# Attention scores of a two-layer trunk: the low part of q on 128 rows beside zeros, and outputs stored block by block

## The chip, the cores and the metric

The kernel runs on one core of one Trainium2 chip. The metric is device time in microseconds (us) for one execution; lower is better. Engines are named as the profile names them: PE is the tensor engine (PEld its weight loads), DVE the vector engine, ACT the scalar engine, POOL GpSimd, SP the engine whose queue (SPq) issues nearly all DMAs here.

## The reference

Two layers over 1024 tokens of 1024 features, each a mixer and then a squared-ReLU MLP with norms around them. The change lies in the scores of two of the four mixers:

```python
def diff_attention(q, k, v, lam, subln_w, rel_bias, layer_idx):      # layer 0: 8 heads, 2 maps of 64 features
    ...
        logits = jnp.einsum("bqhmd,bkhmd->bhmqk", q_blk, k32) + bias[None, :, None]
        logits = jnp.where(dist >= 0, logits, -jnp.inf)
        p = jax.nn.softmax(logits, axis=-1)
        attn = p[:, :, 0] - lam_full * p[:, :, 1]
        return jnp.einsum("bhqk,bkhe->bqhe", attn, v32)
...
def sliding_window_attention(q, k, v, sinks, rel_bias):              # layer 1: 8 heads of 64 features, window 128
    ...
    logits = jnp.einsum("bnqgrd,bnkgd->bngrqk", q32, kb) + bias
```

Everything is fp32. The other two mixers (a state-space scan beside the differential attention, retention beside the sliding window), the projections and the MLPs are untouched.

## The kernel before

A product in fp32 accuracy is made of three products of a faster type: each operand is split into a high part (hi) and the exact rest (lo), and the sum has hi times hi, hi times lo and lo times hi. In the projections (`fm_unit`, L410 to L412, and `tok_unit`, L496 to L498) these are three matmuls on 128 rows with 512 or 256 columns.

A score has only 64 features to contract, so `qk` (L552 to L557) does with two matmuls. `q_stack` (L533) writes hi of q for map m to both halves of the partitions of `qh[:, m]`; `k_stack` (L544) writes hi of k to the map's own 64 partitions and lo of k to the other 64. The first matmul (L555) contracts 128 rows: q hi with k hi and k lo together. The second (L557) has q lo, which stands on the map's own 64 partitions of `ql`, against the hi part of k on the same 64 partitions: it contracts 64 rows. Both accumulate in one tile of PSUM, `psc` in differential attention and `pswa` in the sliding window.

Differential attention (L881 to L943) goes over 8 heads and in each over 8 query blocks of 128, from the last to the first. A block with nk keys has, for each of its 2 maps, one pair of such matmuls for every 512 keys or the rest of them (L903 to L906); then DVE adds the bias and takes the maximum (L909), ACT takes the exponential (L912), DVE joins the maps (L922), PE transposes the result (L929), DVE or ACT copies it to `aT` (L931), PE multiplies by the values (L935), and DVE scales the block into `ys` (L941). `ys` holds all 8 blocks of a head, in slot 16 or 17, and one DMA stores it at the head's end (L943). The `psc` tiles have two buffers of two banks. The projections of the next head and the values of the next pair of heads are issued among the blocks.

The sliding window (L1033 to L1085) goes over 4 pairs of heads and 8 blocks each, with 128 or 256 keys per block, 2 maps, and one matmul pair per map; its outputs were always stored block by block (L1085). There too projections of later heads stand between the blocks.

Each engine's order is set when the program is built: the tile framework places instructions by their dependencies and by when it expects buffers to come free, and then every engine and the SP queue run their list in order. Slots 0 to 19 are 4 KB per partition each and are handed on from phase to phase. GpSimd takes the lo parts of the weights in differential attention and in the sliding window (`lo_on`, L881, L1032, `split_w`, L158).

Of the kernel before, what the change touches and what calls it, by code (L numbers as in the profile page):

```python
# [9 lines left out]
F32 = mybir.dt.float32  # L10
# [18 lines left out]
def trunk(ctx: ExitStack, tc: tile.TileContext, x, c, rel_bias, norm_gains, mod_w, mod_b, mlp_w1, mlp_w2,  # L29
# [13 lines left out]
    def open_wide(shape, bufs):  # L43
        """The other four banks: as two tiles of two banks, or as four of one."""
        if wide:
            wide["stack"].close()
        wide["stack"] = ExitStack()
        wide["pool"] = wide["stack"].enter_context(tc.tile_pool(name="pw", bufs=bufs, space=PSUM, reuse_waits="tile"))
        wide["shape"] = shape
# [10 lines left out]
    def turn(i):  # L60
        """0 and 1 by turns, for each i."""
        turns[i] = 1 - turns.get(i, 1)
        return turns[i]

    def slot(i, shape, dtype=F32, name="slot"):
        """A tile of up to 4 KB in slot i of 20, which the phases of the kernel hand on one by one."""
# [6 lines left out]
    # k_mat: identity, upper triangle (t <= l), strict lower (t > s), ones  # L73
# [29 lines left out]
    def load_cols():  # L103
        """Vectors by feature: cols[:, 0] gains (8 + 8 s), mod_b (40 + 16 s), conv bias (104), SSD norm (120);
        cols[:, 1] conv taps, and the norm of differential attention (64)."""
# [23 lines left out]
    def rstd_of(ss, n, tag="rstd", post=None):  # L129
        """(ss / n + EPS) ** -0.5 on small tiles."""  # L130
# [18 lines left out]
    def split_w(shape, src):  # L149
        """hi by the scalar engine (the next spare[0] by GpSimd), lo by the engine of lo_on."""  # L150
# [16 lines left out]
    def load_fm(w, c0, nft, given=None):  # L167
        """Blocks [128, 8 k, 128 cols] for feature-major products; yields nft (hi, lo) pairs."""
# [10 lines left out]
    def load_group(w, r0):  # L179
        """512 rows of w [*, 1024]: (hi, lo) pairs [128, 2 f, 512] by (f pair, column half)."""  # L180
# [37 lines left out]
    def mod_first(s, after_load, after):  # L218
        """Shift and scale of the first sublayer, 256 columns of each at a time."""
# [7 lines left out]
        for cp in range(4):  # L227
# [11 lines left out]
            # the shift on the tensor engine, as a row; the scale on the vector engine  # L239
# [65 lines left out]
    def col_tasks(s):  # L305
        st = {}

        def fin_t(which):
            def fin(acc):
                col = stat.tile([P, 8], F32, tag=f"col{which}", name="col", bufs=1)  # L310
                parts = split_acc(acc)
                for cc in range(2):
# [3 lines left out]
                    # every row has all the sums: keep the diagonal of each block  # L316
# [10 lines left out]
    xd = {s: dp.tile([NT, P, D], F32, tag=f"xd{s}", name=f"xd{s}") for s in range(3)}  # L327

    class Flow:
        """The residual stream between two sublayers: Y by token tile, u by pairs (hi, lo)."""  # L330
# [23 lines left out]
    def pre_norm(yp, t, xsrc):  # L354
        """Y[t] <- xsrc * rstd(xsrc)."""
# [6 lines left out]
    def post(yp, t, s):  # L362
        """x_new = x + gate * rms(Y) * g_post."""
# [20 lines left out]
    def hT_cols(yp, hf, s, h, ks):  # L384
        """Transposes features ks of the four token tiles of a half, applies (a, b) of sublayer s, splits hi / lo."""
# [18 lines left out]
    def fm_unit(blk, hf):  # L404
        """psum[128 cols, 512 tok] = (W block)^T h of one half."""
# [9 lines left out]
    def out_unit(yp, us, blks, t, cc, first):  # L415
        """Y[t][:, half cc] (+)= sum over 4 f-tiles of u^T w; us[hf][f] = (hi, lo)."""
# [70 lines left out]
    def tok_unit(blks, t, n, ps=None):  # L487
        """psum[128 tok, n cols] = h W for one token tile; blks = [(k0, nk, (hi, lo))]."""
# [24 lines left out]
    def proj_fm(w, c0, nft, evac, early=False, hfs=(0, 1), given=None):  # L513
        """Feature-major product; early: only the first half of the tokens now, the second by what it returns."""
# [13 lines left out]
    def silu2(th, dst, src):  # L528
        """dst = 2 silu(src)."""
# [3 lines left out]
    def q_stack(q, sl, ps):  # L533
        """q = (qh, ql): qh[:, m] has the hi part of one 64-row half of psum / 8 on both halves of the partitions,
        ql the lo parts of the two in place."""
        qh, ql = q
        for m in range(2):
# [3 lines left out]
            nc.vector.scalar_tensor_tensor(out=ql[own, sl], in0=ps[own, :], scalar=0.125,  # L541
# [733 lines left out]
```

## Time and profile before

| | us |
|---|---|
| median of 3 runs | 3244.49 |
| lowest and highest run | 3241.71, 3244.67 |
| span of the profiled execution | 3244.0 |
| differential attention with what is interleaved (480 to 1035) | 555 |
| sliding window with what is interleaved (1953 to 2130) | 177 |

The profiled execution has a span of 3244.0 us, 0.5 us under the median of the runs. The two stages are stretches of that span, from about the first to the last score product of each.

### The profile page before, as it was taken

To read this page: it belongs to the slowest core of one execution; us is meant where nothing else is said; L and a number is where in the kernel's file an instruction comes from. 1 tells how busy PE (TensorE), PEld (TensorE's weight loads), DVE (VectorE), ACT (ScalarE), POOL (GpSimd) and SP (SyncE) were. 2 spreads that over 40 slices of the span, in tenths; PEclk is the share of its full clock that TensorE was granted. 3 is DMA by queue.
4 is the path that set the end of the run, shared out by engine and by line. 5 is a ranking of instruction groups with operands and counts; after the bars stand their busy time and mean duration, and the time that the engine had idled before them with its cause. 6 is when DMAs were issued, how large, how long until landed. Compare 5 with 4: busy or idle time off the path is not lost.

```text
span 3244.0 us, 39799 instructions
## 1 busy us (share of the span) xinstructions
PE 3179.3 (98%) x16018; PEld 2619.1 (81%) x16018; DVE 1696.5 (52%) x3001; ACT 1061.3 (33%) x2041; POOL 456.1 (14%) x414
## 2 busy tenths in 40 slices
PE   8999999999999999999999999999999999999999
PEld 5888887877777878888888878899988788888887
DVE  5788875545675564444433454545455544333334
ACT  4323335444442251112212265432223522111112
POOL 0334442121100120000000142011102100000003
PEclk9999999999999999999999999999999999999999
DMA  6232311111132232322111142233233322111112
GB/s 201 72 101 77 98 53 38 38 54 41 37 143 85 84 124 71 98 91 91 58 47 52 65 146 67 76 109 107 79 130 112 116 78 71 33 47 52 52 52 91
DMA packets 180156, 262.56 MB, mean 81 GB/s; under 512 B 8713, under 2 KB 144514, under 8 KB 179074
## 3 DMA queue, kind: packets, MB, share of 16 engines
q1 hardware_dynamic: 179584, 259.90, 24.5%
q8 instruction: 126, 2.06, 0.3%
q14 instruction: 60, 0.49, 0.0%
q10 hardware_dynamic: 386, 0.11, 0.0%
HBM read 226.95 MB, written 33.03 MB: 80 GB/s over the span
## 4 chain that ended last, share of the span: by engine, by line
PE 86%; DVE 7%; DMA 3%; ACT 2%; issue 1%; POOL 0%; SPq 0%; POOLq 0%; ACTq 0%; DVEq 0%
PE pg L410 11%; PE pg L411 11%; PE pg L412 11%; PE pg L422 10%; PE pg L424 10%; PE pg L423 10%; PE pg L496 4%; PE pg L498 3%; PE pg L497 3%; PE psc L557 2%; PE pav L935 2%; PE psc L555 1%; DVE ch L765 1%; PE pat L929 1%; DMA xt<-xd 1%
## 5 line engine op out<-in xcount | busy, mean ns | idle before, releaser
L410 PE MATMUL pg<-hh,wh 128*128 128x512 f32 x1760 | 693.0, 395 | 5.8 <-ACT hh L393 2.8
L411 PE MATMUL pg<-hl,wh 128*128 128x512 f32 x1760 | 692.9, 394 | 0.1
L412 PE MATMUL pg<-hh,wl 128*128 128x512 f32 x1760 | 692.4, 393 | 0.0
L422 PE MATMUL pg<-wh,u 128*128 128x512 f32 x1472 | 588.0, 400 | 3.1 <-DVE Y L431 2.2
L424 PE MATMUL pg<-wh,u 128*128 128x512 f32 x1472 | 583.6, 397 | 0.0
L423 PE MATMUL pg<-wl,u 128*128 128x512 f32 x1472 | 581.5, 395 | 0.2 <-DVE wl L158 0.2
L156 ACT CAST wh<-raw 128x1024 fp32r<-128x1024 f32 (+1 forms) x246 | 257.3, 1049 | 797.9 <-PE pg L424 546.7
L410 PEld LDWEIGHTS pg<-hh,wh 128*128 128x128 f32 x1760 | 330.6, 188 | 79.8 <-ACT hh L393 4.2
L412 PEld LDWEIGHTS pg<-hh,wl 128*128 128x128 f32 x1760 | 330.9, 188 | 70.3 <-issue 2.1
L411 PEld LDWEIGHTS pg<-hl,wh 128*128 128x128 f32 x1760 | 331.1, 188 | 69.6 <-issue 2.3
L158 DVE TENSOR_TENSOR wl<-raw,wh 128x1024 fp32r<-128x1024 f32 (+1 forms) x194 | 238.1, 1230 | 256.4 <-ACT wh L156 256.3
L422 PEld LDWEIGHTS pg<-wh,u 128*128 128x128 f32 x1472 | 277.8, 189 | 69.1 <-DVE Y L431 4.1
L431 DVE TENSOR_TENSOR Y<-pg,Y 128x512 f32<-128x512 f32 x264 | 181.9, 689 | 290.0 <-PE pg L424 287.6
L424 PEld LDWEIGHTS pg<-wh,u 128*128 128x128 f32 x1472 | 277.4, 189 | 66.4 <-issue 0.6
L423 PEld LDWEIGHTS pg<-wl,u 128*128 128x128 f32 x1472 | 277.9, 189 | 64.1 <-DVE wl L158 0.5
L496 PE MATMUL pg<-wh,hh 128*128 128x256 f32 (+1 forms) x992 | 292.5, 295 | 13.7 <-DVE zs L531 11.5
L498 PE MATMUL pg<-wh,hl 128*128 128x256 f32 (+1 forms) x992 | 288.4, 291 | 0.6 <-DVE hl L395 0.6
L497 PE MATMUL pg<-wl,hh 128*128 128x256 f32 (+1 forms) x992 | 288.5, 291 | 0.0
L368 POOL TENSOR_TENSOR yg<-Y,gg 128x512 f32<-128x512 f32 x36 | 54.8, 1522 | 1344.0 <-DVE Y L431 1343.0
L496 PEld LDWEIGHTS pg<-wh,hh 128*128 128x128 f32 x992 | 192.6, 194 | 18.5 <-DVE zs L531 10.9
L498 PEld LDWEIGHTS pg<-wh,hl 128*128 128x128 f32 x992 | 192.2, 194 | 4.8 <-issue 1.4
L497 PEld LDWEIGHTS pg<-wl,hh 128*128 128x128 f32 x992 | 192.7, 194 | 3.1 <-issue 1.0
(327 smaller groups left out, 3906.3 us busy)
## 6 DMA issues: line engine op xcount, KB each, us to landing
raw<-in_mlp_w_dram SPq DMA_DIRECT2D x64, 1024.0 KB, 5.3
raw<-in_mod_w_dram SPq DMA_DIRECT2D x40, 1024.0 KB, 5.0
raw<-in_e_w_in_dram SPq DMA_DIRECT2D x32, 512.0 KB, 4.0
xd<-xt SPq DMA_DIRECT2D x24, 512.0 KB, 2.6
xt<-xd SPq DMA_DIRECT2D x24, 512.0 KB, 4.3
raw<-in_e_w_in_dram SPq DMA_DIRECT2D x10, 1024.0 KB, 5.5
raw<-in_e_w_out_dram SPq DMA_DIRECT2D x10, 1024.0 KB, 5.6
raw<-in_o_w_in_dram SPq DMA_DIRECT2D x9, 1024.0 KB, 5.2
```

The lines of the kernel that those rows point to most:

```text
L156: nc.scalar.copy(out=wh, in_=src)
L158: lo_on[0].tensor_tensor(out=wl, in0=src, in1=wh.bitcast(F32), op=ALU.subtract)
L410: mm(ps, lhsT=wh[:, k], rhs=hh[:, k], start=(k == 0), stop=False)
L411: mm(ps, lhsT=wh[:, k], rhs=hl[:, k], start=False, stop=False)
L412: mm(ps, lhsT=wl[:, k], rhs=hh[:, k], start=False, stop=(k == 7))
L422: mm(ps, lhsT=uh[:, tl], rhs=wh[:, f % 2], start=(f == 0), stop=False)
L423: mm(ps, lhsT=uh[:, tl], rhs=wl[:, f % 2], start=False, stop=False)
L424: mm(ps, lhsT=ul[:, tl], rhs=wh[:, f % 2], start=False, stop=(f == 3))
L431: nc.vector.tensor_tensor(out=dst, in0=ps, in1=dst, op=ALU.add)
L496: mm(ps[:, 0:n], lhsT=hh[:, k, tl], rhs=wh[:, i], start=(k == 0), stop=False)
L497: mm(ps[:, 0:n], lhsT=hh[:, k, tl], rhs=wl[:, i], start=False, stop=False)
L498: mm(ps[:, 0:n], lhsT=hl[:, k, tl], rhs=wh[:, i], start=False, stop=(k == 7))
```

## The change

The second score product contracts 128 rows: each map has its own `ql` tile, with the lo part of q on the map's 64 partitions and zeros on the other 64, and the stationary and moving operands of L557 become whole 128-partition slices. `q_tiles` clears the other half with a GpSimd memset of 64 partitions by 1024 columns, twice per head in differential attention and twice per pair of heads in the sliding window (24 in all). In differential attention the second `ql` tile takes slots 16 and 17; `ys` becomes a tile of one block with three buffers, stored at each block (64 stores of 128 by 128 instead of 8 of a whole head), and `aT` has three buffers instead of four. In the sliding window the second `ql` tile takes slot 15 or the buffer `macc`, which is otherwise the accumulator of the modulation vectors. Comments and docstrings are gone too, so lines after L556 have other numbers.

```diff
     def q_stack(q, sl, ps):
...
-            nc.vector.scalar_tensor_tensor(out=ql[own, sl], in0=ps[own, :], scalar=0.125,
+            nc.vector.scalar_tensor_tensor(out=ql[m][own, sl], in0=ps[own, :], scalar=0.125,
                                            in1=qh[own, m, sl].bitcast(F32), op0=ALU.mult, op1=ALU.subtract)
...
         qh, ql = q
         mm(ps, lhsT=qh[:, m, qsl], rhs=ks[:, ksl], start=True, stop=False)
-        rows_ = slice(m * 64, m * 64 + 64)
-        mm(ps, lhsT=ql[rows_, qsl], rhs=ks[rows_, ksl], start=False, stop=True)
+        mm(ps, lhsT=ql[m][:, qsl], rhs=ks[:, ksl], start=False, stop=True)
+
+    def q_tiles(qh, ql):
+
+        for m in range(2):
+            nc.gpsimd.memset(ql[m][64 - m * 64:128 - m * 64, :].bitcast(F32), 0.0)
+        return [(qh[i], [t[:, i * 512:i * 512 + 512] for t in ql]) for i in range(2)]
...
-                places = ((12, 13, 2, 3, 4), (19, 18, 14, 15, 5))[h % 2]
-                ql = slot(places[4], [P, D], F32R, "ql")
-                q = [(slot(places[2 * i], [P, 2, 512], F32R, "qh"), ql[:, i * 512:i * 512 + 512]) for i in range(2)]
+                places = ((12, 13, 2, 3, 4, 16), (19, 18, 14, 15, 5, 17))[h % 2]
+                q = q_tiles([slot(places[2 * i], [P, 2, 512], F32R, "qh") for i in range(2)],
+                            [slot(places[4 + m], [P, D], F32R, "ql") for m in range(2)])
...
-                ys = slot(16 + h % 2, [P, 8, P], F32, "ys")
...
-                        aT = mp.tile([P, 4, P], F32, tag="aT", name="aT", bufs=4)
+                        aT = mp.tile([P, 4, P], F32, tag="aT", name="aT", bufs=3)
...
-                    nc.vector.tensor_scalar(out=ys[:, qb], in0=po[:, 0:P], scalar1=r, scalar2=rc[:, 0:1],
+                    ys = mp.tile([P, P], F32, tag="ys", name="ys", bufs=3)
+                    nc.vector.tensor_scalar(out=ys, in0=po[:, 0:P], scalar1=r, scalar2=rc[:, 0:1],
                                             op0=ALU.mult, op1=ALU.mult)
-                nc.sync.dma_start(out=yd[2 + h // 4][:, :, (h % 4) * P:(h % 4 + 1) * P], in_=ys)
+                    nc.sync.dma_start(out=yd[2 + h // 4][:, qb, (h % 4) * P:(h % 4 + 1) * P], in_=ys)
...
-                ql = slot(places[2], [P, D], F32R, "ql")
-                q = [(slot(places[n], [P, 2, 512], F32R, "qh"), ql[:, n * 512:n * 512 + 512]) for n in range(2)]
+                lo1 = slot(15, [P, D], F32R, "ql") if i % 2 == 0 else const.tile([P, D], F32R, tag="macc", name="ql")
+                q = q_tiles([slot(places[n], [P, 2, 512], F32R, "qh") for n in range(2)],
+                            [slot(places[2], [P, D], F32R, "ql"), lo1])
```

What the program's order becomes is shown at three places. The first is PE in the second head of differential attention, before the change (score products L555 and L557, values times probabilities L935, projections L410 to L412, a transposition L929; a size is that of the output):

```order
L555 MATMUL psc<-ks,qh 128x512
L557 MATMUL psc<-ks,ql 128x512
L935 MATMUL pav<-v,aT 128x128 x2
L555 MATMUL psc<-ks,qh 128x512
L557 MATMUL psc<-ks,ql 128x512
L410 MATMUL pg<-hh_595,wh 128x512
L555 MATMUL psc<-ks,qh 128x512
L557 MATMUL psc<-ks,ql 128x512
L555 MATMUL psc<-ks,qh 128x384
L929 MATMUL pat<-kmat,p 128x128
L557 MATMUL psc<-ks,ql 128x384
```

The same place on PE with the change (L556 is the second product, L939 and L933 are what were L935 and L929):

```order
L555 MATMUL psc<-ks,qh 128x512
L556 MATMUL psc<-ks,ql 128x512
L939 MATMUL pav<-v,aT 128x128 x2
L555 MATMUL psc<-ks,qh 128x512
L556 MATMUL psc<-ks,ql 128x512
L410 MATMUL pg<-hh_595,wh 128x512
L555 MATMUL psc<-ks,qh 128x512
L556 MATMUL psc<-ks,ql 128x512
L555 MATMUL psc<-ks,qh 128x384
L556 MATMUL psc<-ks,ql 128x384
L933 MATMUL pat<-kmat,p 128x128
```

The order is the same but for one transposition, which stands behind the second product now.

The second place is the SP queue in the first heads of differential attention, before (L163 loads weights of 256 or 128 columns to `raw`, L677 a bias tile, L943 stores a head):

```order
L163 DMA raw<-in_e_w_in_dram 128x8x128
L943 DMA ye_400<-ys 1024x1x128
L163 DMA raw<-in_e_w_in_dram 128x8x256
L163 DMA raw<-in_e_w_in_dram 128x8x128 x2
L677 DMA bt_4027<-vd 128x256
L943 DMA ye_400<-ys 1024x1x128
```

And the SP queue there with the change (L682 is the bias tile, L948 the store of a block):

```order
L163 DMA raw<-in_e_w_in_dram 128x8x128
L948 DMA ye_400<-ys 128x128 x5
L163 DMA raw<-in_e_w_in_dram 128x8x256
L163 DMA raw<-in_e_w_in_dram 128x8x128
L948 DMA ye_400<-ys 128x128 x2
L163 DMA raw<-in_e_w_in_dram 128x8x128
L948 DMA ye_400<-ys 128x128
L682 DMA bt_4027<-vd 128x256
```

Stores stand between the loads of the weights now, one to five at a time, where one store per head stood behind all loads of a head.

The third place is GpSimd over one head, before (L158 takes lo parts of weights, L135 is the small power of a norm, one per query block):

```order
L158 TENSOR_TENSOR wl<-raw,wh 128x1024
L135 TENSOR_TENSOR rs<-ms,expo 128x1 x5
L158 TENSOR_TENSOR wl<-raw,wh 128x1024 x2
L135 TENSOR_TENSOR rs<-ms,expo 128x1
L158 TENSOR_TENSOR wl<-raw,wh 128x1024
```

And with the change (L561 clears half of a `ql` tile):

```order
L158 TENSOR_TENSOR wl<-raw,wh 128x1024
L561 MEMSET ql 64x1024
L135 TENSOR_TENSOR rs<-ms,expo 128x1
L158 TENSOR_TENSOR wl<-raw,wh 128x1024
L561 MEMSET ql 64x1024
L135 TENSOR_TENSOR rs<-ms,expo 128x1 x5
L158 TENSOR_TENSOR wl<-raw,wh 128x1024 x2
```

The two memsets of a coming head stand among the lo parts of weights and the powers of the head that runs.

## Rows read from the trace of the kernel before

**Rows 1.** The page's first part: busy time, share of the span, instructions.

```profile
PE 3179.3 (98%) x16018; PEld 2619.1 (81%) x16018; DVE 1696.5 (52%) x3001; ACT 1061.3 (33%) x2041; POOL 456.1 (14%) x414
```

**Rows 2.** Chain that ended last, 480 to 1035 us, shares by line.

```profile
by line: PE psc L557 12.2%; PE pav L935 12.0%; PE pg L410 10.0%; PE pg L412 9.9%; PE pg L411 9.6%; PE psc L555 8.6%; PE pat L929 5.7%; PE pg L498 4.7%; PE pg L496 4.6%; PE pg L497 4.4%; PE pg L422 4.2%; PE pg L423 4.1%; PE pg L424 4.0%; ACT
```

**Rows 3.** Windows: length, busy PE, PEld, DVE, ACT, POOL, granted clock, DMA, GB/s.

```profile
480.00:1035.00 555.00, 545.10 (x2868) 425.05 (x2866) 316.55 (x814) 262.42 (x607) 94.58 (x91) 0.99 0.17 54
1953.00:2130.00 177.00, 177.00 (x1048) 147.47 (x1047) 96.70 (x305) 86.98 (x243) 24.71 (x14) 1.00 0.23 70
```

**Rows 4.** Line L557 in `psc`: durations in ns, first and last start, forms.

```profile
L557 PE MATMUL psc<-ks,ql x192: 322/466/507, 484.5 to 1019.7; 64*128 64x512 f32 x96, 64*128 64x384 f32 x32, 64*128 64x256 f32 x32, 64*128 64x128 f32 x32
```

**Rows 5.** Timeline, 690 to 703: start, us, engine, line, rows*columns, moving shape, idle before.

```profile
698.72 0.40 PE L555 MATMUL psc<-ks,qh 128*128 128x512 f32 x1
...
699.04 0.18 PEld L557 LDWEIGHTS psc<-ks,ql 64*128 64x128 f32 x1 [0.26 <-issue]
699.05 0.49 PE L557 MATMUL psc<-ks,ql 64*128 64x512 f32 x1
...
699.47 0.39 PE L555 MATMUL psc<-ks,qh 128*128 128x256 f32 x1
...
699.78 0.38 PE L557 MATMUL psc<-ks,ql 64*128 64x256 f32 x1
...
700.10 0.39 PE L498 MATMUL pg<-wh,hl 128*128 128x256 f32 x1
...
701.00 0.28 PE L498 MATMUL pg<-wh,hl 128*128 128x256 f32 x1
701.00 0.19 PEld L496 LDWEIGHTS pg<-wh,hh 128*128 128x128 f32 x1
...
701.12 0.28 PE L496 MATMUL pg<-wh,hh 128*128 128x256 f32 x1
```

**Rows 6.** Timeline, 480 to 500: later pairs of a group.

```profile
485.40 0.50 PE L557 MATMUL psc<-ks,ql 64*128 64x512 f32 x1
...
485.83 0.50 PE L555 MATMUL psc<-ks,qh 128*128 128x512 f32 x1
...
486.26 0.50 PE L557 MATMUL psc<-ks,ql 64*128 64x512 f32 x1
```

**Rows 7.** Timeline of PE, 738 to 752: two projection matmuls of 512 columns.

```profile
739.43 0.40 PE L412 MATMUL pg<-hh,wl 128*128 128x512 f32 x1
739.66 0.40 PE L410 MATMUL pg<-hh,wh 128*128 128x512 f32 x1
```

**Rows 8.** Timeline of PE, 2126 to 2140: a score pair of the sliding window.

```profile
2127.21 0.28 PE L555 MATMUL pswa<-ks,qh 128*128 128x256 f32 x1
2127.42 0.38 PE L557 MATMUL pswa<-ks,ql 64*128 64x256 f32 x1
2127.72 0.38 PE L498 MATMUL pg<-wh,hl 128*128 128x256 f32 x1
2127.95 0.28 PE L496 MATMUL pg<-wh,hh 128*128 128x256 f32 x1
```

**Rows 9.** Timelines, DVE's and PE's: first and last of 64 blocks, L922 and transposes.

```profile
491.16 1.29 DVE L922 SCALAR_TENSOR_TENSOR p<-p,rc 128x1024 f32<-128x1024 f32 x1
...
496.22 1.09 PE L929 MATMUL pat<-kmat,p 128*128 128x128 f32 x8
...
1022.03 0.35 DVE L922 SCALAR_TENSOR_TENSOR p<-p,rc 128x128 f32<-128x128 f32 x1
...
1026.31 0.27 PE L929 MATMUL pat<-kmat,p 128*128 128x128 f32 x1
```

**Rows 10.** Line L866: the nearest memset on GpSimd, durations in ns.

```profile
L866 POOL MEMSET bt<- x2: 738/738/738, 485.6 to 486.2; 128x768 f32 x2
```

**Rows 11.** Line L1085, the sliding window's stores of 128 by 128: issue to landing.

```profile
DMA to landing us min/median/max: 1.5/1.6/5.2
```

**Rows 12.** Waits of the SP queue, 480 to 1035: total us, times, longest.

```profile
SPq L163 <- POOL wl L158: 182.0, 16, 41.3
```

## The prediction

> **What bounds the kernel now.** I read the page's busy times first, then the chain of waits over differential attention, then the windows of the two stages with scores, and last the timeline around single score products. PE is busy for 98% of the span and DVE, the next, for 52% [rows 1]. A busy PE alone proves little, since its matmuls overlap, but the chain over 480 to 1035 us consists of PE lines almost throughout, with the second score product L557 at its head: 12.2%, against 8.6% for the first one, L555, which has the same columns on twice the rows [rows 2]. In that window PE is busy 545 of 555 us, DVE 317, ACT 262, POOL 95; in the sliding window PE fills all 177 us and DVE 97 [rows 3]. The clock is granted at 0.99 and 1.00, so neither stage has clock to win. Time taken from PE there is time taken from the end, as long as the others keep up.
>
> **What a score pair costs now.** Durations mislead here; what counts is the distance from one start to the next. Two projection matmuls of 512 columns on 128 rows start 0.23 us apart [rows 7], two of 256 columns 0.12 us (701.00 to 701.12), and the weight load of the later one starts together with the matmul ahead of it [rows 5]. Around L557 it is otherwise. Its weight load starts only at 699.04, after 0.26 us in which the load path waited for nothing that the profile shows, and the matmul starts with it at 699.05. The pair of 512 columns takes 0.33 + 0.42 = 0.75 us (698.72, 699.05, 699.47), the pair of 256 behind it 0.31 + 0.32 = 0.63 (699.47, 699.78, 700.10) [rows 5]. A later pair of 512 in a group takes 0.43 + 0.43 = 0.86 [rows 6]. So where the number of rows changes, the next weights are loaded only when the matmul ahead is nearly through (699.04, against its end at 699.12), not beside it. The first matmul after a group pays as well: its follower starts 0.23 us later (2127.72 to 2127.95) where 0.12 is usual [rows 8].
>
> **What the change takes away.** With both products on 128 rows I price each at the usual distance: a pair of 512 at 0.46, of 256 at 0.24. Counts in differential attention are 96 pairs of 512 and 32 each of 384, 256 and 128 [rows 4]; in the sliding window the code gives 4 x 8 x 2 = 64 pairs, 8 of them of 128 columns and 56 of 256.
> - 512: 0.75 - 0.46 = 0.29 at a group's head, 0.86 - 0.46 = 0.40 later. Groups of both kinds are common; I take 0.34: 96 x 0.34 = 32.6 us (27.8 to 38.4).
> - 256: 0.63 - 0.24 = 0.39: 12.5 us.
> - 384: between the two, 0.37: 11.8 us (9.3 to 12.8).
> - 128: no row of its own; an estimate between half and all of the 256 figure, nearer the lower end since the load itself (0.19 us) then fills much of the distance: 0.22, 7.0 us (6.2 to 12.5).
> - Sliding window: 0.21 + 0.30 - 0.24 = 0.27 at a group's head [rows 8], 0.39 as above later; 0.31 x 56 = 17.4 us, and 8 x 0.2 = 1.6 (together 16.7 to 25).
> - The matmul after a group: 0.23 - 0.12 = 0.11. Going through the whole timeline I count 126 groups in the first stage and 47 in the second: 173 x 0.11 = 19.0 us (0 to 19).
>
> The sum is 63.9 + 19.0 + 19.0 = 102 us; from the ends, 72 to 120.
>
> One rule speaks against this. TensorE: Matmul & The Clock Gate (the Trainium skill), Part 3, under "What overlaps and what doesn't", says that a weight load overlaps a running matmul only where the two use different row groups. By it two products on all 128 rows could not hide the second load, and a pair would win nothing. The rows at 701.00 say otherwise: L496's load starts with L498's matmul, both on 128 rows, and the next matmul comes 0.12 us later, less than the load's own 0.19 [rows 5]. By the rule the sum is 0, by the row 102; I go by the row.
>
> **What is given back.** PE's order around the scores stays (the first place shown), so the work that stands between a block's scores and its transposes shrinks, while DVE and ACT need as long as before. For each of the 64 blocks I took the time from the end of L922 to the first transpose: 496.22 - 492.45 = 3.8 us in the first, 1026.31 - 1022.38 = 3.9 us in the last [rows 9], 4.6 in the median, 0.06 in three. Against that I set 0.42 us for each score pair that stands between the block's own last product and its transposes. In six blocks this is more than the slack; the excess adds up to 7 us. The same for `psc`, which has two buffers (its next product against the end of the exponential two tiles before), gives 3 to 4 us. In the sliding window no block's slack is exceeded. So 11 us come back as waits. The last head has less to put between its blocks than the others: 3 us more, with 0 and the 10 us that PE lacks of its window now [rows 3] as ends.
>
> **The added work.** 24 memsets: 128x768 takes 0.74 us [rows 10], so 1024 columns about 0.98, 24 us in all on POOL. Sixteen fall in the first stage, where POOL is busy 95 of 555 us; what hides them is that idle time. What waits behind a memset on POOL is a lo part of weights or a block's power; nothing from below (a gain) has a reason. I take 0, with 24 us as the upper end. The first head's second `ql` stands in slot 16, which the scan before it uses for its decays, so its q projections move behind the scan's end; the values' projections take their place. I take 2 us (0 to 5.5, a unit of 24 matmuls at 0.23).
>
> Stores: 56 more on the SP queue, of the size that the sliding window stores in 1.6 us [rows 11]; bytes are the same. `aT` with three buffers: a block has at most two, and in the order the products with the first follow before the next block's transposes, so 0. `macc` and slot 15 in the sliding window hold up the next modulation sums until its last scores; they feed a gate and a norm needed far later: 0.
>
> **Sum.** 102 - 11 - 3 - 2 = 86 us. The profiled span is 3244.0, so 3158; the median of the runs lies 0.5 above: **3159 us**. The likeliest case reaches from 3141 (all of 102 kept) to 3185 (72 less the 13 that come back).
>
> **Rivals.**
> - *DVE and ACT set the pace* (0.12). With 70 us less, DVE would be busy 317 of about 485 us in differential attention, 65%, and ACT 54%. If each of the 64 blocks waited 0.7 us more than the slack says, because what precedes on DVE and ACT is late too, 43 us come back: about 3200. For it: three blocks have no slack. Against it: the median slack is 4.6 us, and DVE's own work would start earlier as well.
> - *The pair keeps its price* (0.05): the second load does not run beside the first product on 128 rows either, because both read the same keys or add to one tile. Then nothing is won: 3244, give or take 5. Against it: projections add 24 products to one tile at 0.23 us [rows 7]. The page's rule above would come out here.
> - *Slower, by the SP queue* (0.04). A load L163 already waits at the head of the queue for POOL, 182 us in 16 waits, 41.3 at the longest [rows 12]. Now stores stand behind such loads. `ys` has three buffers; at 8.3 us a block (531 us from the first of 64 to the last [rows 9]) they last 25 us. A wait of 41 us would hold DVE, and soon PE, 16 us; once a head that is 128 us: 3244 - 86 + 128 = 3286. It decides from 11 us a head on. Against it: the load's wait is that for a buffer whose release comes at PE's pace, and the order places stores ahead of loads that come free later.
> - *More than forecast* (0.05): the later pairs' 0.40 throughout and no waits, under 3141.
>
> **Chances and range.** The forecast has 0.74. A change of 0.2% (6.5 us) is about what a measurement of this kernel can tell from none. Faster: 0.74 + 0.12 + 0.05 = 0.91; same 0.05; slower 0.04. From 3141 to 3195 lies the forecast and a good part of the first rival, 0.8 together.
>
> **What would show it.** Right: L556 on 128 rows, pairs of 512 starting about 0.23 us apart, no "issue" before their loads; the first stage about 65 us shorter, the sliding window about 22; PE's waits in the first stage up from 10 us to some 20 to 25. Wrong: pairs still 0.4 us apart (the second rival); PE waits of 50 us or more on L912 or L922 (the first); DVE waiting at `ys` for a DMA (the third).

## The result, and the profile after

The changed kernel takes 3169.53 us (median of 4 runs, 3167.74 to 3171.93) against 3244.58 us for the kernel before (4 runs, 3241.71 to 3249.16). The ratio is 0.9763 with a 95% interval of 0.9746 to 0.9781: 75 us less. The profiled execution has a span of 3165.9 us, 78.1 less than before. The range held it; the point of 3159 was 10.5 us too low, and the reason for these 10 us is the more useful part of what follows.

The page's first part, busy time by engine, answers to [rows 1]:

```profile
PE 3089.8 (98%) x16018; PEld 2606.5 (82%) x16018; DVE 1688.8 (53%) x2994; ACT 1059.4 (33%) x2048; POOL 479.2 (15%) x438
```

PE has the same 16018 matmuls and is busy 89.5 us less. Its share of the span is 98% as it was, so PE still sets the end.

The second product alone, by form (durations in ns, minimum, median, maximum, then first and last start), answers to [rows 4]:

```profile
L556 PE MATMUL psc<-ks,ql x192: 272/377/480, 486.8 to 957.7; 128*128 128x512 f32 x96, 128*128 128x384 f32 x32, 128*128 128x256 f32 x32, 128*128 128x128 f32 x32
```

Every second product runs on 128 rows. From the first to the last of them are 470.9 us (486.8 to 957.7), where L557 took 535.2 (484.5 to 1019.7).

The timeline around the first score group, weight loads and matmuls (answers to [rows 6]):

```profile
486.39 0.19 PEld L555 LDWEIGHTS psc<-ks,qh 128*128 128x128 f32 x1
...
486.61 0.39 PE L555 MATMUL psc<-ks,qh 128*128 128x512 f32 x1
486.62 0.19 PEld L556 LDWEIGHTS psc<-ks,ql 128*128 128x128 f32 x1
486.84 0.40 PE L556 MATMUL psc<-ks,ql 128*128 128x512 f32 x1
486.84 0.19 PEld L555 LDWEIGHTS psc<-ks,qh 128*128 128x128 f32 x1
487.07 0.40 PE L555 MATMUL psc<-ks,qh 128*128 128x512 f32 x1
```

Matmul follows matmul at 0.23 us (486.61, 486.84, 487.07), and each load starts together with the matmul ahead of it and is over (486.81) before that matmul ends (487.00). No score load of after is preceded by idle time put down to "issue". This is the distance of the projections in [rows 7], and a load does run beside a matmul that uses the same 128 rows. The rule of the Trainium skill that the prediction weighed (TensorE: Matmul & The Clock Gate, Part 3, "What overlaps and what doesn't") says otherwise; the trace does not agree with it, by 0.23 us between starts.

The sliding window shows the same with 256 columns (timeline of PE, answers to [rows 8]):

```profile
2011.96 0.28 PE L555 MATMUL pswa<-ks,qh 128*128 128x256 f32 x1
2012.08 0.28 PE L556 MATMUL pswa<-ks,ql 128*128 128x256 f32 x1
2012.19 0.28 PE L555 MATMUL pswa<-ks,qh 128*128 128x256 f32 x1
2012.31 0.28 PE L556 MATMUL pswa<-ks,ql 128*128 128x256 f32 x1
2012.43 0.39 PE L411 MATMUL pg<-hl,wh 128*128 128x512 f32 x1
```

Four products take 0.47 us (2011.96 to 2012.43), where one pair took 0.51 before [rows 8] (2127.21 to 2127.72).

The windows of the two stages with scores (columns as in [rows 3]):

```profile
480.00:958.00 478.00, 467.53 (x2830) 411.20 (x2830) 299.95 (x782) 256.89 (x599) 109.28 (x101) 1.00 0.20 64
1887.00:2037.00 150.00, 150.00 (x1022) 137.35 (x1021) 78.90 (x282) 78.35 (x232) 27.00 (x17) 1.00 0.17 49
```

In the first stage PE lacks 10.5 us of its window. The window of [rows 3] goes on for 15 us behind the last score product; cut at that product, as here, PE lacked 7.7 us before:

```profile
480.00:1019.80 539.80, 532.07 (x2807) 414.62 (x2805) 307.90 (x794) 256.35 (x593) 92.93 (x88) 0.99 0.17 54
```

So little of the work that went was replaced by waits. In the sliding window PE lacks nothing.

The clock is a small part of this stage's difference. Before, the stage has two stretches of 3.4 us at the lower clock level (0.50, 1.2 GHz), from 910.1 and from 957.9; after has none in its stage. Ahead of the first PE was busy 2.66 of 4.00 us (906 to 910). That stretch, in the windows of before:

```profile
910.10:913.50 3.40, 3.40 (x11) 2.85 (x12) 2.57 (x7) 0.29 (x2) 0.00 (x0) 0.50 0.72 292
```

Projections of 512 columns start 0.43 us apart there instead of 0.23, so the two stretches cost about 3.2 us (an estimate: 2 x 3.4 x (1 - 0.23/0.43)). All six traces of this study in which the first stage has 64-row products show such stretches in it, 6.8 to 23.8 us in all; the three with 128 rows (after and experiments 2 and 4) show none. Why, no run shows. Over the whole execution the mean granted clock is 0.992 before and after, so the 78 us as a whole are not the clock's.

Cutting each execution at the starts of certain matmuls shows where the time went. Each column is a distance between two such starts in the trace, in us: PE's start to the first score product of differential attention; from there to the last; to the first of the sliding window; to its last; to the last product of retention scores (`pret`); to PE's last matmul.

| | to first | diff. attention | to sliding window | sliding window | to end of retention scores | rest |
|---|---|---|---|---|---|---|
| before | 480.2 | 535.5 | 933.4 | 175.9 | 261.4 | 845.4 |
| after | 482.8 | 471.1 | 929.3 | 150.3 | 273.5 | 846.9 |
| difference | +2.6 | -64.4 | -4.1 | -25.6 | +12.1 | +1.5 |

The two stages became 90 us shorter together. The stretch right behind the sliding window, which no line of the diff touches, became 12.1 us longer. 1.9 us of that are 16 matmuls of 256 columns (0.12 each) that stood inside the sliding window before and stand behind it now (1039 and 1023 matmuls there). The rest is a stall. The waits of PE, 2037 to 2310 (total us, times, longest), name it:

```profile
PE pret L1121 <- DVE ys L1089: 4.2, 1, 4.2
PE pg L496 <- ACT v L988: 2.4, 1, 2.4
```

And the timeline of that place, DVE, the SP queue and PE, shows how it arises (L279 and L281 sum a modulation vector in `macc`, L163 loads weights of a projection, L1089 and L1091 write and store a block of the sliding window's output):

```profile
2037.31 0.29 PE L556 MATMUL pswa<-ks,ql 128*128 128x256 f32 x1
...
2038.20 0.75 DVE L279 TENSOR_SCALAR macc<-raw,cact 128x1024 f32<-128x1024 f32 x1
...
2040.89 1.27 DVE L281 SCALAR_TENSOR_TENSOR macc<-raw,cact,macc 128x1024 f32<-128x1024 f32 x1
...
2042.08 0.28 DVE L1089 TENSOR_TENSOR ys<-pswa,mxs 128x128 f32<-128x128 f32 x1
2042.18 0.38 SPq L163 DMA_DIRECT2D raw<-in_o_w_in_dram  x1
...
2042.66 0.53 SPq L1091 DMA_DIRECT2D yo<-ys  x1
...
2043.03 1.27 DVE L281 SCALAR_TENSOR_TENSOR macc<-raw,cact,macc 128x1024 f32<-128x1024 f32 x1
2043.34 0.60 PE L1113 MATMUL pkz<-kmat,qk 128*128 128x128 f32 x4
...
2044.36 1.26 DVE L281 SCALAR_TENSOR_TENSOR macc<-raw,cact,macc 128x1024 f32<-128x1024 f32 x1
2045.54 0.28 DVE L1089 TENSOR_TENSOR ys<-pswa,mxs 128x128 f32<-128x128 f32 x1
...
2047.54 1.99 ACT L156 CAST wh<-raw 128x1024 fp32r<-128x1024 f32 x2 [5.88 <-DMA raw<-in_o_w_in_dram]
2047.84 0.29 DVE L1089 TENSOR_TENSOR ys<-pswa,mxs 128x128 f32<-128x128 f32 x1 [2.03 <-DMA yo<-ys]
...
2048.19 1.21 PE L1121 MATMUL pret<-qk 128*128 128x128 f32 x4 [4.25 <-DVE ys L1089]
```

Read it from top to bottom. For the last pair of heads `macc` holds the lo part of q, so the modulation sum can't begin before the last score product has read it, at 2037.31. The sum follows at once, with L279 at 2038.20 and three L281 of 1.27 us. While it was held up, its two loaded tiles of weights stayed in the `raw` ring. The load L163 (1 MB) starts at 2042.18, right after the second of these operations ends (2040.89 + 1.27 = 2042.16). The store of the block written at 2042.08 is issued right behind it, at 2042.66, only 0.3 us after its block was ready. But it lands late. Line L1091 in 2042.6 to 2044, where it has this one store, and the DMA queue's packets from 2042.6 to 2046.5:

```profile
DMA to landing us min/median/max: 5.1/5.1/5.1
q1 hardware_dynamic: 879, 0.90, 74.6%
```

The median of these stores is 1.6 us. The 879 packets are 0.90 MB, so all of them have the 1024 bytes of a row of L163; a row of the store has 512. None of the store's data had started by 2046.5: they moved behind the load's. The sliding window's `ys` has two buffers, so the last block, which DVE writes at 2047.84, needs the buffer of just this store: that is the 2.03 us of idle time, up to the landing at 2047.72. Only then is the PSUM tile free for the first product of the next stage: PE stands still for 4.25 us, until 2048.19. ACT has waited 5.88 us for the same load. The 2.4 us of the second PE wait lie behind ACT too: it gets to the result at 2059.27, behind a cast that waited 6.68 us for the next load L163.

One more loss hangs on the stall. Windows of after around it:

```profile
2043.00:2048.00 5.00, 0.94 (x9) 0.70 (x8) 2.97 (x8) 0.46 (x1) 0.00 (x0) 1.00 0.91 289
2048.30:2051.60 3.30, 3.24 (x14) 2.95 (x15) 2.99 (x3) 2.40 (x4) 0.00 (x0) 0.50 1.00 371
2051.70:2056.00 4.30, 4.30 (x35) 4.20 (x34) 3.28 (x5) 0.00 (x0) 0.00 (x0) 1.00 0.63 186
```

When PE starts again the granted clock is 0.50, its lower level (1.2 GHz), for the 3.3 us of the second window, and 1.00 after. Fourteen matmuls take these 3.3 us; in the third window 35 take 4.3, so fourteen would take 1.7, and about 1.6 us are lost (an estimate, since the matmuls are not all of the same size). Together 4.25 + 2.4 + 1.6 + 1.9 = 10.2 of the 12.1 us; the last 2 I could not assign to single rows, but experiment 4 shows that they go with `macc` as well.

### The profile page after: what moved, and what is told of

Read it like the earlier page. It is cut to its first block, busy times and chain, and to the rows that moved or that the text cites. A ratio compares the mean times of both kernels' runs of the same rounds, so it can differ in the third digit from the quotient of the medians.

```text
span 3165.9 us, 40016 instructions
## 1 busy us (share of the span) xinstructions
PE 3089.8 (98%) x16018; PEld 2606.5 (82%) x16018; DVE 1688.8 (53%) x2994; ACT 1059.4 (33%) x2048; POOL 479.2 (15%) x438
## 4 chain that ended last, share of the span: by engine, by line
PE 83%; DVE 8%; DMA 4%; ACT 3%; issue 1%; POOL 1%; SPq 0%; POOLq 0%; ACTq 0%; DVEq 0%
PE pg L410 11%; PE pg L411 11%; PE pg L412 11%; PE pg L422 10%; PE pg L424 10%; PE pg L423 10%; PE pg L496 3%; PE pg L498 3%; PE pg L497 3%; PE pav L939 2%; DVE ch L770 1%; PE psc L555 1%; PE psc L556 1%; PE pat L933 1%; DMA raw<-in_mod_w_dram 1%
## 5 line engine op out<-in xcount | busy, mean ns | idle before, releaser
L410 PE MATMUL pg<-hh,wh 128*128 128x512 f32 x1760 | 689.9, 393 | 6.0 <-ACT hh L393 2.8
L412 PE MATMUL pg<-hh,wl 128*128 128x512 f32 x1760 | 691.0, 393 | 0.3 <-DVE ms L133 0.3
L410 PEld LDWEIGHTS pg<-hh,wh 128*128 128x128 f32 x1760 | 330.7, 188 | 76.5 <-ACT hh L393 4.1
L412 PEld LDWEIGHTS pg<-hh,wl 128*128 128x128 f32 x1760 | 331.0, 188 | 67.7 <-DVE wl L158 0.7
L158 DVE TENSOR_TENSOR wl<-raw,wh 128x1024 fp32r<-128x1024 f32 (+1 forms) x194 | 238.0, 1230 | 256.7 <-ACT wh L156 256.5
L496 PEld LDWEIGHTS pg<-wh,hh 128*128 128x128 f32 x992 | 192.8, 195 | 20.3 <-DVE zs L531 11.0
L135 POOL TENSOR_TENSOR rs<-ms,expo 128x1 f32<-128x1 f32 x160 | 102.6, 642 | 618.1 <-DVE ms L133 595.3
```

Of the source, the lines that this page charges most:

```text
L158: lo_on[0].tensor_tensor(out=wl, in0=src, in1=wh.bitcast(F32), op=ALU.subtract)
L410: mm(ps, lhsT=wh[:, k], rhs=hh[:, k], start=(k == 0), stop=False)
L412: mm(ps, lhsT=wl[:, k], rhs=hh[:, k], start=False, stop=(k == 7))
L496: mm(ps[:, 0:n], lhsT=hh[:, k, tl], rhs=wh[:, i], start=(k == 0), stop=False)
```

## The experiments

The theory after this look: the gain is the price of switching between 128 and 64 rows, about 90 us; `macc` costs about 10; memsets, block stores and three `aT` cost nothing. Rivals: that what the change adds (memsets, stores, slots) costs in its own right, and that 64 rows are slow by themselves, not the switch.

**1. Everything but the 128 rows.** The memsets, the second `ql` tiles, `macc`, the stores by block and three `aT` stay, but the second product contracts 64 rows again:

```diff
+        rows_ = slice(m * 64, m * 64 + 64) if rows else slice(0, 128)
...
-        mm(ps, lhsT=ql[m][:, qsl], rhs=ks[:, ksl], start=False, stop=True)
+        mm(ps, lhsT=ql[m][rows_, qsl], rhs=ks[rows_, ksl], start=False, stop=True)
...
```

(`rows` is an argument of `qk` that both calls set to True here.)

> All of the change but the rows: the second score product reads its own 64 rows of the new ql tiles; memsets, slots, block stores and three aT buffers stay. Theory (the gain is the change of the row count, and the rest costs only what follows the sliding window): between 3244 and 3257, pairs of 512 columns 0.75 to 0.86 us as before. Rival (a good part of the 75 us comes from the new order, the block stores or the smaller aT): below 3225.

Measured: 3255.21 us (3251.43 to 3260.54) against 3246.91 for before in the same comparison; ratio 1.003, 1.0019 to 1.004. So the rest of the change costs about 8 us and wins nothing; the gain lies in the 128 rows. The stretch behind the sliding window is 272.8 us long, nearly that of after (273.5), and the wait is there, in the waits of PE from 2030 to 2400:

```profile
PE pret L1122 <- DVE ys L1090: 4.4, 1, 4.4
```

**2. Differential attention alone.** The sliding window is as before:

```diff
-                lo1 = slot(15, [P, D], F32R, "ql") if i % 2 == 0 else const.tile([P, D], F32R, tag="macc", name="ql")
-                q = q_tiles([slot(places[n], [P, 2, 512], F32R, "qh") for n in range(2)],
-                            [slot(places[2], [P, D], F32R, "ql"), lo1])
+                ql = slot(places[2], [P, D], F32R, "ql")
+                q = [(slot(places[n], [P, 2, 512], F32R, "qh"), [ql[:, n * 512:n * 512 + 512]] * 2) for n in range(2)]
...
```

> The change in differential attention alone; the sliding window has its 64-row products and one ql tile as before, and macc is the accumulator's alone. Theory: the first stage keeps its 64 us, nothing is lost behind the sliding window: 3244.6 - 66 = 3179, between 3172 and 3186, and PE waits for nothing long at the first retention scores. Rival (the 12 us behind the sliding window come with any new order of the program): about 3190 or more.

Measured: 3180.99 us (3179.21 to 3181.97), ratio 0.9801, 0.9785 to 0.9818: 66 us less than before. Its first stage is 471.0 us, that of after, and the stretch behind the sliding window 261.4, that of before. As expected.

**3. The sliding window alone,** with slot 15 and `macc` as in the change; differential attention with `ys` for a whole head, one `ql` and 64 rows:

```diff
-                places = ((12, 13, 2, 3, 4, 16), (19, 18, 14, 15, 5, 17))[h % 2]
...
+                places = ((12, 13, 2, 3, 4), (19, 18, 14, 15, 5))[h % 2]
+                ql = slot(places[4], [P, D], F32R, "ql")
...
+                ys = slot(16 + h % 2, [P, 8, P], F32, "ys")
...
-                        aT = mp.tile([P, 4, P], F32, tag="aT", name="aT", bufs=3)
+                        aT = mp.tile([P, 4, P], F32, tag="aT", name="aT", bufs=4)
...
```

> The change in the sliding window alone, with macc for the odd pairs of heads; differential attention as before. Theory: its stage 24 us shorter, 12 us lost behind it: 3244.6 - 12 = 3232, between 3227 and 3238. Rival (macc costs nothing, the loss belongs to the other stage): 3220.

Measured: 3229.37 us (3227.43 to 3233.95), ratio 0.9954, 0.9939 to 0.9969. Its sliding window is 150.3 us long, 25.6 shorter, but the whole kernel only 17.5 (3246.91 - 3229.37): the stretch behind it takes 271.3 us where before took 261.4. The gain of 17.5 (10 to 20 by the interval) is more than the 12 expected, but not clearly so. Again the wait stands there (PE, 2030 to 2400):

```profile
PE pret L1122 <- DVE ys L1090: 3.3, 1, 3.3
```

**4. The change without `macc`.** The second `ql` tile of the sliding window takes slots 15, 14, 15 and 9 for the four pairs of heads; nothing else is altered:

```diff
-                lo1 = slot(15, [P, D], F32R, "ql") if i % 2 == 0 else const.tile([P, D], F32R, tag="macc", name="ql")
+                lo1 = slot((15, 14, 15, 9)[i], [P, D], F32R, "ql")
```

> The changed kernel, but in the sliding window the second ql tile of the odd pairs of heads takes slots 14 and 9, not macc. Theory (the ql tile in macc holds the modulation sums, these a raw buffer and the loads and stores behind it in the SP queue, and so the first retention scores): the wait of 4 us at the first retention scores and the low clock behind it go, 3169.5 - 10 = 3159, between 3154 and 3164. Rival (the loss is one of fillers: with the sliding window shorter there is too little PE work to cover its last blocks, whatever buffer ql has): 3167 to 3172.

Measured: 3158.57 us (3155.36 to 3160.57), ratio to before 0.9733, 0.9718 to 0.9747; that is 11 us less than after, and the fastest version of this study. The two come from different comparisons: each against its own before, this one is 88.3 us faster and after 75.1. The traces give the effect by itself: the sliding window and the stretch behind it take 152.2 + 261.4 = 413.6 us where after takes 150.3 + 273.5 = 423.8, which is 10.2 less. (The 16 projection matmuls stand inside the sliding window again, 1039 as before.) The windows of the place where after stands still show PE at work throughout (columns as in [rows 3]):

```profile
2044.00:2055.00 11.00, 11.00 (x99) 11.00 (x98) 2.88 (x14) 4.09 (x14) 0.20 (x1) 1.00 0.31 77
```

After, over its own stall:

```profile
2044.00:2055.00 11.00, 6.75 (x42) 6.46 (x43) 8.12 (x13) 3.16 (x4) 0.00 (x0) 0.84 0.85 288
```

The stretch behind the sliding window is 261.4 us, as before, and no wait of PE on L1089 is left in it.

**5. The rest of the change, without `macc`.** Experiment 1 with the slots of experiment 4; it shows what memsets, block stores and three `aT` cost alone:

```diff
-        mm(ps, lhsT=ql[m][:, qsl], rhs=ks[:, ksl], start=False, stop=True)
+        mm(ps, lhsT=ql[m][rows_, qsl], rhs=ks[rows_, ksl], start=False, stop=True)
...
-                lo1 = slot(15, [P, D], F32R, "ql") if i % 2 == 0 else const.tile([P, D], F32R, tag="macc", name="ql")
+                lo1 = slot((15, 14, 15, 9)[i], [P, D], F32R, "ql")
```

> All of the change but the rows, as in the run of the rest alone, and with the second ql tile of the odd pairs in slots 14 and 9. Theory (macc alone makes the rest cost 9 us; memsets, block stores and three aT buffers are nearly free): 3244.6 + 2, between 3241 and 3250, and no wait of 4 us at the first retention scores. Rival (memsets and stores cost it): 3252 or more.

Measured: 3246.21 us (3242.89 to 3251.34) against 3248.08; ratio 0.9997, 0.9988 to 1.0006. Nothing, within 0.1%. The memsets are there (by form, in ns):

```profile
L562 POOL MEMSET ql<- x24: 944/947/955, 344.0 to 2043.3; 64x1024 f32 x24
```

24 of 0.947 us are 22.7 us on POOL, and POOL's idle time hides all of them. Between experiments 1 and 5 only the place of that `ql` tile differs: 3255.21 - 3246.21 = 9 us (10 when each is taken against its own before), in a kernel that has none of the gain.

**6. The switch, or the 64 rows?** Before, but in blocks with more than 512 keys the two first products of a map stand together, and then its two second ones, still on 64 rows:

```diff
-                        for n0 in range(0, nk, 512):
-                            n1 = min(n0 + 512, nk)
-                            qk(ps[:, n0:n1], q[qb // 4], m, ks[n0 // 512][:, m],
-                               slice(qb % 4 * P, qb % 4 * P + P), slice(0, n1 - n0))
+                        for part in range(2):
+                            for n0 in range(0, nk, 512):
+                                n1 = min(n0 + 512, nk)
+                                qk(ps[:, n0:n1], q[qb // 4], m, ks[n0 // 512][:, m],
+                                   slice(qb % 4 * P, qb % 4 * P + P), slice(0, n1 - n0), part)
```

> The kernel before, with one edit: in a block of more than 512 keys the two first products of a map are issued, then its two second products, which stay on 64 rows. Theory (what costs is the change of the row count): two changes per map instead of four; the second 64-row product starts about 0.23 us after the first one of 512 columns, and 64 maps at 0.3 to 0.4 us save 19 to 26 us: 3244.6 - 22 = 3223, between 3217 and 3230. Rival (a product on 64 rows is slow in itself): the two 64-row products still start 0.43 us apart, and less than 10 us are saved.

Measured: 3225.5 us (3222.53 to 3231.92), ratio 0.9933, 0.9919 to 0.9946. Half of the switches of these blocks are gone and 22.6 us with them by the medians (17.5 to 26.3 by the interval), though all 64-row products are still there: the switch has a price. The profiled execution, at 3231.92 the slowest of the four, has a first stage of 520.3 us, 15.2 less than before; it has 23.8 us at the lower clock level in that stage, where before has 6.8, and that costs it some 8 us by the same estimate as above. The time is as the theory expected, the spacing isn't. Timeline around the first group (rows of two matmuls are one row, x2):

```profile
486.05 0.62 PE L556 MATMUL psc<-ks,qh 128*128 128x512 f32 x2
...
486.60 0.29 PEld L559 LDWEIGHTS psc<-ks,ql 64*128 64x128 f32 x2 [0.36 <-issue]
486.60 0.72 PE L559 MATMUL psc<-ks,ql 64*128 64x512 f32 x2
...
487.25 0.30 PEld L556 LDWEIGHTS psc<-ks,qh 128*128 128x128 f32 x2 [0.36 <-issue]
487.25 0.73 PE L556 MATMUL psc<-ks,qh 128*128 128x512 f32 x2
...
487.92 0.73 PE L559 MATMUL psc<-ks,ql 64*128 64x512 f32 x2
```

Two products on 128 rows and the switch to 64 take 0.55 us (486.05 to 486.60); two on 64 rows and the switch back take 0.65 (486.60 to 487.25). In the trace the second 64-row product starts 0.336 us after the first one (median; both on the same 64 rows), not 0.23 as expected. That alone would speak for the rival that 64 rows are slow by themselves. The next pair shows that they are not: it is on 128 rows, stands behind a switch too, and takes 0.67 with the switch that follows (487.25 to 487.92), and its row lasts 0.73 us as that of a 64-row pair does (0.72), where the 128-row pair with no switch ahead lasts 0.62. The starts in this trace from 480 to 1030 say the same, each as a median and for products of 512 columns whose predecessor has more than 128. A 128-row product is followed by another after 0.337 us when its predecessor is on 64 rows (45 cases), and after 0.229 when it isn't (968). A 64-row product that follows another one hands over to 128 rows in 0.323 us (15 cases), no later than a 128-row product that follows 128 rows hands over to 64 (0.327, 18 cases). So the theory stands: what costs is the switch, and it costs twice, about 0.1 us where the row count changes and 0.1 more on the start after that, in either direction. The second part is the price of "the matmul after a group" in the prediction.

**7. Two maps side by side.** Before, but in blocks of up to 512 keys the first products of both maps come first, then the second ones of both, each on its own 64 rows:

```diff
+                    if nk <= 512:
+                        for part in range(2):
+                            for m in range(2):
+                                qk(both[:, m, 0:nk], q[qb // 4], m, ks[0][:, m],
+                                   slice(qb % 4 * P, qb % 4 * P + P), slice(0, nk), part)
...
```

(The loop behind it leaves these blocks out.)

> The kernel before, with one edit: in the 32 blocks of up to 512 keys the first products of both maps are issued, then the second products of both, each on its own 64 of the 128 partitions. In the grouped run two 64-row products on the same partitions started 0.34 us apart. If a weight load waits only for a matmul that uses the same rows, the second of the two starts well under 0.34 us after the first for 512 columns and 0.12 us or less for 256. If any load behind a 64-row matmul waits, it starts 0.34 us behind for 512 columns and some 0.23 for 256. Time: 3246 less 32 blocks at 0.3 to 0.6 us, 3227 to 3238, in either case.

Measured: 3231.92 us (3229.46 to 3232.59) against 3244.4; ratio 0.9957, 0.9941 to 0.9974, about 12 us less and within what was expected for either case. Timeline of PE at two such groups:

```profile
520.78 0.51 PE L556 MATMUL psc<-ks,qh 128*128 128x384 f32 x2
521.21 0.44 PE L559 MATMUL psc<-ks,ql 64*128 64x384 f32 x2
521.58 0.39 PE L497 MATMUL pg<-wl,hh 128*128 128x256 f32 x1
...
526.66 0.40 PE L556 MATMUL psc<-ks,qh 128*128 128x256 f32 x2
526.98 0.39 PE L559 MATMUL psc<-ks,ql 64*128 64x256 f32 x2
527.30 0.39 PE L498 MATMUL pg<-wh,hl 128*128 128x256 f32 x1
```

The two 64-row products of a group start 0.004 us apart in the trace (median over all four shapes) and are both through in 0.39 us at 256 columns: on different halves they run at the same time. The Trainium skill says this in TensorE: Matmul & The Clock Gate, Part 3, under "The mechanism", where products on different row groups start about 4 ns apart; the trace agrees. Even so the pair does not pay: from 526.98 to 527.30 it holds PE for 0.32 us, and the two products on 128 rows that the change puts in its place take 0.24 (2 x 0.12). The pair takes as long as one 64-row product of that size between products of 128 rows (0.311, the median of before): both switches are still paid.

## Why the prediction came out as it did

**The price of a pair: right in mechanism, 9 us too large in the first stage.** The medians are close to what the prediction used: 0.239 and 0.233 us for the two products of 512 columns (before 0.367 and 0.428). The first stage's score products, each counted from its start to the next matmul's, add up to 134.7 us before and 78.7 after, 56.0 less; forecast 63.9. By columns: 512 gave 27.1 (32.6 forecast), 384 gave 8.1 (11.8), 256 gave 11.3 (12.5), 128 gave 9.5 (7.0). What is missing at 512 and 384 are starts that come later than the median: 41 products of 512, nearly all first ones, are followed only after 0.31 to 0.34 us, and four groups end with a gap of 0.7 to 1.4 us (3.3 us beyond the usual distance, waits that are counted here). All of the 41 stand right behind a matmul of 128 columns (L933, L939, L620), and of the 145 that don't none is so late; projections of 512 columns behind one of 128 hold their follower as long (0.315). That is 3.5 us of the 32.6, which the prediction, going by the usual distance, left out. The matmul after a group gave 13.2 us (its follower's distance, 33.5 us summed before and 20.3 after); 126 x 0.11 = 13.9 was forecast. There are 118 groups in place of 126 now, so a part of the 13.2 is that there are fewer. The sliding window gave 18.7 of 19.0, and its followers 3.6 of 5.2. Together 91.5 us in place of 102.

**What comes back as waits: too large.** I set 11 us for slack, 3 for the last head and 2 for slot 16. The first stage lost 56.0 + 13.2 = 69.2 us around its score products and became 64.4 shorter with 12 more matmuls in it (2798 and 2786), which are 1.4 to 2.8 us at 0.12 to 0.23. The stretches at the lower clock, about 3.2 us before and none after, are in the 64.4 as well; the prediction read the 0.99 of [rows 3] as no clock to win. So 5 to 7 us came back besides the 3.3 of these gaps, 8 to 10 together, where 14 were forecast for this stage. Less of it than forecast is waits: PE lacks 10.5 us of the window, not 20 to 25, and 7.7 of the same stretch before; the rest I could not assign. The waits of PE there, 480 to 960:

```profile
PE pav L939 <- ACT aT L935: 5.3, 6, 1.2
PE pat L933 <- ACT aT L935: 1.5, 2, 0.8
PE psc L555 <- ACT p L916: 1.1, 4, 0.4
```

Blocks wait a little more for `aT` and less for `psc`. Why so little comes back is argued, not shown: I set each block's slack against the work that went, as if DVE and ACT began no earlier, while their own inputs come earlier too, as the text on that rival says itself. This error and the one above (102 for 91.5) nearly cancel. The 2 us of slot 16 fall ahead of the stage; that stretch is 2.6 us longer, but 1.4 to 2.0 longer also in the three experiments that leave the slot as it was (3, 6 and 7), so the term is not shown by itself.

**Memsets, stores, `aT` at 0: right** (experiment 5). A memset took 0.947 us; the estimate was 0.98. In after 12 of the 24 start between 480 and 958, not 16. The lower end of the range was a little off, too: with all of 102 kept the sum gives 3142, not 3141.

**The step that failed** is the sentence that `macc` and slot 15 "hold up the next modulation sums until its last scores; they feed a gate and a norm needed far later: 0". No row speaks against the second half, that the result is needed late. But I followed the sum forward to its reader and not back to what it holds: two `raw` tiles, and with them the loads that need these tiles, which now come at the moment in which the last blocks are stored. And the sum's own DVE work, 0.75 + 3 x 1.27 us of it, comes in one lump into the moment in which DVE has to empty the last PSUM tiles. The place of that tile cost about 10 us (experiment 4 against after, and experiment 1 against 5). How much of PE's 4.25 us would remain without the lump no run shows: it delays the block before the last (its product ends at 2043.50, it is written at 2045.54), but in this trace the wait ends with the landing of the store at 2047.72, behind the data of the load.

**The rivals.** *DVE and ACT set the pace:* no, PE lacks 2.7 us more of the first stage than before, not 43. *The pair keeps its price:* no, by the spacing. *Slower, by the SP queue:* a part of its chain came about, in the sliding window in place of differential attention, and once: the `ys` ring ran full, and PE waited 4 us, not 16 a head. But the store was not held at its issue by a load that waited for a buffer (0.3 us); its data stood behind the load's. Where I had looked for it, the waits of the SP queue (480 to 960) show less than before [rows 12]:

```profile
SPq L948 <- DVE ys L946: 233.5, 40, 16.2
SPq L163 <- POOL wl L158: 61.9, 17, 10.8
```

The queue now waits mostly at the stores, for the block itself. Loads wait for POOL at most 10.8 us, less than the 25 us that the ring of three `ys` lasts.

**The sum as it came out:** 64.4 + 25.6 from the two stages, less the 12.1 behind the sliding window; the other columns of the table cancel (2.6 - 4.1 + 1.5 = 0). That is 77.9 of the 78.1 us between the spans. Without `macc` the span is 3157.4, 86.6 less than before, where 86 was forecast; the agreement is in part luck, since two errors nearly cancel.

## What to carry to other kernels

A product that contracts 64 rows among products of 128 costs more than its columns say: here a pair at 512 columns went from 0.8 to 0.47 us when the operand was filled up with zeros, and the fill cost nothing on an idle engine. Read the distance between starts, not durations, to see it. When a buffer is borrowed from another phase, follow both ways what waits for it: who needs the result, and what the waiting instruction keeps occupied (buffers, and through them loads) while it waits, and what meets those loads when they start late.

## What the runs showed of the hardware beyond what was expected

- Behind a change of the row count, in either direction, the first product of 512 columns holds the next one on the same rows for 0.337 us instead of 0.23 (experiment 6); two 64-row products on different halves start 0.004 us apart (experiment 7).
- A product of 512 columns right behind a matmul of 128 columns holds its follower 0.315 us instead of 0.23, on 128 rows throughout (after).
- A store of 64 KB issued 0.48 us behind a load of 1 MB on the same queue took 5.06 us to land, 1.6 being the median of its kind; its data moved behind the load's (after).
- After PE had 0.94 us of work in 5 us (2043 to 2048), the granted clock was 0.50 for 3.3 us: a stall of 4.25 us cost about 1.6 more. In the kernel without the stall it was 1.00 there.
